# Three pairs of feed-forward input units by seven block products each, with the second matrix's chunks between them

## The chip, the cores and the metric

One core of one Trainium2 chip runs the kernel. The metric is the device time of one execution in microseconds. A core has a matrix engine (TensorE, PE in the rows; PEld is its weight loading), a vector engine (VectorE, DVE), a scalar engine (ScalarE, ACT), GpSimd (POOL), a queue that issues transfers (SyncE, SP), an on-chip memory SBUF, and a small memory PSUM of eight banks into which TensorE writes its sums.

## The reference

x has 256 rows (tokens) of 1024 columns, in float32. Two layers follow each other, each with a feed-forward, a mixer (attention in the first layer, retention in the second) and a second feed-forward:

```python
def _swiglu(xn, w_in, w_out):
    a, b = jnp.split(xn @ w_in, 2, axis=-1)
    return (jax.nn.silu(a) * b) @ w_out
...
        h = x + 0.5 * _swiglu(_rms(x, ffn1_norm[i]), ffn1_w_in[i], ffn1_w_out[i])
        xn = _rms(h, mix_norm[i])
...
        h = h + m.astype(h.dtype)
        x = h + 0.5 * _swiglu(_rms(h, ffn2_norm[i]), ffn2_w_in[i], ffn2_w_out[i])
```

In a feed-forward `w_in` is 1024 x 5632 (2816 columns for a, 2816 for b) and `w_out` 2816 x 1024. The four feed-forwards are called f0 to f3 here: f0, attention, f1, f2, retention, f3.

## The kernel before, in words

**Precision.** Each float32 operand of a large product is split in two numbers of TensorE's faster format: hi, its rounding, and lo, the rest. A product of two operands is three matmuls: hi by hi, lo by hi, hi by lo (`mm_tokens`, L280). A matmul has 128 rows of the left operand held in the array, and 512 columns of the right one streamed through it.

**Weights.** The class `Weights` (L96) keeps a list of loads in the order in which they are used. A load is one `raw` tile of 128 x 2048 float32 (1 MB), brought by SP. ACT rounds it to `hi` (L162), in two pieces of 128 x 1024, and DVE subtracts to get `lo` (L169). There are four raw, four hi and four lo buffers. Loads run ahead of the splits (L128), and splits at most four parts ahead of the parts that TensorE has freed (L151). While matmuls are issued, the object `Flow` (L61) counts the nanoseconds that TensorE should take, and issues one split piece every 800 of them (L174) unless `urgent` is set, which is so around a norm. A step of side work is a generator that yields the nanoseconds after which it goes on. The program's order is what these counts give; the scheduler that compiles the program may still put instructions of an engine in another order, where their inputs allow (only SP's order and the opening's are held, L801 and L486).

**A feed-forward** (`ffn`, L437) has eleven units of 256 columns of a and the 256 columns of b that belong to them. A unit takes two parts: rows 0 to 511 and 512 to 1023 of its 512 columns of `w_in`. For each of two groups of 128 tokens it sums 24 matmuls in one PSUM bank (`ps_f`), after which ACT takes the silu (`st_f`, L442) and DVE multiplies (`gt_f`, L444). Two transposes on TensorE (`ptg_f`, L305) and another split give `hT`, the left operand of the second matrix. When all units are done, `out_proj` (L384) goes through the second matrix in eleven chunks of 256 rows, one part each; four banks (`y`) hold the 256 x 1024 result, 24 matmuls a chunk. The last two chunks are taken together, tile by tile, so that the residual (L423), the squares (L345), the root on POOL (L355), the scaling (`xs`, L369), four transposes per 512 columns and the split into `xn` (`norm_transpose`, L361) can begin before the last tile is summed. The next stage's first matmuls follow.

The diff touches `Weights`, the plan of loads (`plan_ffn`, L243), `norm_transpose`, `out_proj`, `ffn` and the calls at the end (L795).

Of the kernel before, what the change touches and what calls it, by code (L numbers as in the profile page):

```python
# [15 lines left out]
ALU = mybir.AluOpType  # L16
# [79 lines left out]
class Weights:  # L96

    RAW, PARTS, PACE = 4, 4, 800  # L100

    def __init__(self, nc, pool, flow):
        self.nc, self.pool, self.flow = nc, pool, flow
        self.specs, self.raws, self.parts = [], [], []
        self.taken = self.freed = self.next = 0
        self.todo, self.rounded = [], []
        flow.idle = self.paced

    def add(self, src, shape, pieces):
        self.specs.append((src, shape, pieces))  # L110

    def cols(self, w, c0, n, k0=0, nk=KD, pieces=2):
        src = w[k0 * P : (k0 + nk) * P, c0 : c0 + n].rearrange("(k p) c -> p k c", p=P)
        self.add(src, [nk, n], pieces)

    def pair_cols(self, w, c0, c1, n, k0, nk, pieces=2):
# [4 lines left out]
        self.add(src, [nk, 2 * n], pieces)  # L121

    def rows(self, w, k0):
        src = w[k0 * P : (k0 + 2) * P, :].rearrange("(k p) c -> p k c", p=P)
        self.add(src, [2, w.shape[1]], 2)

    def load(self, most=1000):
        while len(self.raws) < min(len(self.specs), len(self.parts) + self.RAW, most):  # L128
            i = len(self.raws)
            src, shape, pieces = self.specs[i]  # L130
            raw = self.pool.tile([P] + shape, F32, tag="raw", name=f"raw{i}", bufs=self.RAW)
            n = shape[0] // (pieces if pieces > 2 else 1)
            parts = src if isinstance(src, list) else [src]
# [6 lines left out]
            self.raws.append(raw)  # L140

# [6 lines left out]
    def round(self):  # L148
        if not self.todo:
# [4 lines left out]
            _, shape, pieces = self.specs[i]  # L154
# [7 lines left out]
        self.nc.scalar.copy(self.parts[i][0][:, ks, :], self.raws[i][:, ks, :])  # L162
        return True

    def remain(self):
        i, ks, last = self.rounded.pop(0)
        hi, lo = self.parts[i]
        raw = self.raws[i]
        self.nc.vector.tensor_tensor(lo[:, ks, :], raw[:, ks, :], hi[:, ks, :], ALU.subtract)  # L169
        if last:  # L170
            self.raws[i] = None
            self.load()
# [32 lines left out]
def trunk_kernel(ctx: ExitStack, tc: tile.TileContext, io, out: bass.AP):  # L205
# [36 lines left out]

    def plan_ffn(w_in, w_out):  # L243
        for j in range(FF // 256):
            for i in range(2):
                pieces = 2 if len(wts.specs) > 1 else 4
                wts.pair_cols(w_in, j * 256, FF + j * 256, 256, 4 * i, 4, pieces)
        for c in range(FF // 256):
# [25 lines left out]
    def mm(ps, lhsT, rhs, start, stop):  # L274
        nc.tensor.matmul(ps, lhsT=lhsT, rhs=rhs, start=start, stop=stop)  # L275
# [4 lines left out]
    def mm_tokens(ps, t, part, k0, nk, first, last):  # L280

        hi, lo = part
        for k in range(nk):
# [4 lines left out]
            mm(ps, xh, lo[:, k, :], False, last and k == nk - 1)  # L288

# [36 lines left out]
    def sum_halves(out_ap, ps, name):  # L326
        rest = work.tile([P, T], F32, tag="rest", name=f"rest_{name}")
# [33 lines left out]
    def norm_transpose(t, dst, gain, name):  # L361
# [3 lines left out]
        xs = []  # L365
        for n in range(2):
            x = work.tile([P, 512], F32, tag="xs", name=f"xs_{name}{t}{n}")
# [462 lines left out]
```

## Time and profile before

| | us |
|---|---|
| three runs, median (lowest to highest) | 1081.95 (1081.24 to 1082.28) |
| the profiled execution | 1081.91 |
| its span, first to last instruction | 1080.1 |
| TensorE busy | 1070.1 |
| VectorE busy | 622.6 |
| ScalarE busy | 512.5 |

A profile is one execution. In its rows L162 is line 162 of the kernel, `hi<-raw` an instruction that writes hi and reads raw, x24 a count, and what stands in brackets the idle time before it and what ended it. Matmuls overlap, so the mean of one is longer than the distance from start to start; the distance is what counts for the time. Some matmul records are missing from a trace. The granted clock is 1.00 at TensorE's full 2.4 GHz.

### The profile page before, as it was taken

What the parts mean: (1) busy time and instruction counts of PE and PEld (TensorE: products, weight loads), DVE (VectorE), ACT (ScalarE), POOL (GpSimd) and SP (SyncE); (2) the same over time, 40 slices, a digit from 0 to 9 for tenths busy, and PEclk for the clock granted to TensorE, in tenths of its full rate; (3) what the DMA queues carried; (4) which work ended last, traced back from release to release, by engine and by line L of the source; (5) the groups of instructions that cost most, each with busy time, mean ns of one, the idle gap of its engine ahead of it and who ended that gap; (6) DMA issues with size and microseconds to landing.
All of it is one profiled execution on the core that took longest, in us unless ns stands there. A gap on an engine that the chain in (4) does not pass through costs nothing.

```text
span 1080.1 us, 12936 instructions
## 1 busy us (share of the span) xinstructions
PE 1070.1 (99%) x5016; PEld 878.1 (81%) x5016; DVE 622.6 (58%) x848; ACT 512.5 (47%) x789; POOL 37.2 (3%) x38
## 2 busy tenths in 40 slices
PE   8999999999999999999999999999999999999998
PEld 6888888877778888888888888888888888888887
DVE  5646544778875655546554554656655556565541
ACT  6545443557664444434444543445544444454430
POOL 0000000122010000000000000000000000000000
PEclk9999999999999999999999999999999999999999
DMA  8965555473337565564756465476456556656531
GB/s 282 284 194 159 205 186 194 138 242 124 121 118 243 170 203 173 194 195 137 234 181 203 162 201 193 142 242 205 154 177 217 156 156 198 191 163 205 181 115 39
DMA packets 135440, 196.47 MB, mean 182 GB/s; under 512 B 5330, under 2 KB 104658, under 8 KB 135379
## 3 DMA queue, kind: packets, MB, share of 16 engines
q1 hardware_dynamic: 135378, 195.65, 56.5%
q8 instruction: 39, 0.64, 0.2%
q14 instruction: 23, 0.18, 0.0%
HBM read 194.58 MB, written 1.05 MB: 181 GB/s over the span
## 4 chain that ended last, share of the span: by engine, by line
PE 94%; DVE 3%; POOL 1%; issue 1%; SPq 0%; DMA 0%; ACT 0%; POOLq 0%; ACTq 0%
PE ps_f L275 44%; PE pj L275 13%; PE y_f3o L275 6%; PE y_f1o L275 6%; PE y_f0o L275 6%; PE y_f2o L275 6%; PE pqk L275 4%; PE y_rto L275 4%; PE ptg_f L305 2%; PE y_dao L275 2%; DVE lo L169 1%; PE rpo L686 1%; PE po L611 0%; PE sT L665 0%; DMA raw<-in_ffn_w_in_dram 0%
## 5 line engine op out<-in xcount | busy, mean ns | idle before, releaser
L169 DVE TENSOR_TENSOR lo<-raw,hi 128x1024 fp32r<-128x1024 f32 (+1 forms) x364 | 430.5, 1209 | 242.0 <-ACT hi L162 241.3
L162 ACT CAST hi<-raw 128x1024 fp32r<-128x1024 f32 (+1 forms) x364 | 367.4, 1043 | 256.6 <-PE ps_f L275 95.2
L275 PE MATMUL ps_f<-hi,xn_in 128*128 128x512 f32 x352 | 113.4, 402 | 1.4 <-ACT xn_in L323 1.4
L275 PE MATMUL ps_f<-hi,xn_dao 128*128 128x512 f32 x352 | 111.1, 396 | 0.0
L275 PE MATMUL ps_f<-hi,xn_rto 128*128 128x512 f32 x352 | 111.1, 396 | 0.0
L275 PE MATMUL ps_f<-hi,xn_f1o 128*128 128x512 f32 x352 | 111.1, 396 | 0.0
L442 ACT ACTIVATE st_f<-ps_f 128x256 f32<-128x256 f32 x88 | 33.3, 378 | 134.2 <-PE ps_f L275 134.2
L444 DVE TENSOR_TENSOR gt_f<-ps_f,st_f 128x256 f32<-128x256 f32 x88 | 36.9, 420 | 87.5 <-ACT st_f L442 87.5
L275 PE MATMUL pj<-hi,xn_f2o 128*128 128x512 f32 x256 | 81.1, 393 | 0.0
L275 PEld LDWEIGHTS ps_f<-hi,xn_in 128*128 128x128 f32 x352 | 66.0, 192 | 15.3 <-ACT xn_in L323 1.8
L275 PEld LDWEIGHTS ps_f<-hi,xn_dao 128*128 128x128 f32 x352 | 64.7, 188 | 12.7
L275 PEld LDWEIGHTS ps_f<-hi,xn_f1o 128*128 128x128 f32 x352 | 64.7, 188 | 12.7
L275 PEld LDWEIGHTS ps_f<-hi,xn_rto 128*128 128x128 f32 x352 | 64.7, 188 | 12.7
L275 PE MATMUL ps_f<-lo,xn_in 128*128 128x512 f32 x176 | 69.8, 397 | 0.0
L275 PE MATMUL ps_f<-lo,xn_f1o 128*128 128x512 f32 x176 | 68.9, 392 | 0.0
L275 PE MATMUL ps_f<-lo,xn_rto 128*128 128x512 f32 x176 | 68.9, 391 | 0.0
L275 PE MATMUL ps_f<-lo,xn_dao 128*128 128x512 f32 x176 | 68.9, 391 | 0.0
L275 PE MATMUL pj<-hi,xn_f0o 128*128 128x512 f32 x192 | 62.6, 400 | 0.0
L275 PE MATMUL y_f3o<-hi,hT_f 128*128 128x512 f32 (+1 forms) x220 | 56.9, 348 | 0.0
L275 PEld LDWEIGHTS pj<-hi,xn_f2o 128*128 128x128 f32 x256 | 48.1, 188 | 9.7
L275 PE MATMUL y_f0o<-hi,hT_f 128*128 128x512 f32 x176 | 54.8, 391 | 0.0
L275 PE MATMUL y_f1o<-hi,hT_f 128*128 128x512 f32 x176 | 54.7, 391 | 0.0
(189 smaller groups left out, 1519.7 us busy)
## 6 DMA issues: line engine op xcount, KB each, us to landing
raw<-in_ffn_w_in_dram SPq DMA_DIRECT2D x172, 512.0 KB, 5.0
raw<-in_ffn_w_out_dram SPq DMA_DIRECT2D x44, 1024.0 KB, 4.9
raw<-in_rt_w_in_dram SPq DMA_DIRECT2D x24, 1024.0 KB, 5.2
raw<-in_da_w_in_dram SPq DMA_DIRECT2D x12, 1024.0 KB, 5.1
raw<-in_rt_w_out_dram SPq DMA_DIRECT2D x8, 1024.0 KB, 5.0
raw<-in_da_w_out_dram SPq DMA_DIRECT2D x4, 1024.0 KB, 4.9
raw<-in_ffn_w_in_dram SPq DMA_DIRECT2D x16, 128.0 KB, 3.7
g_in_ffn_norm_dram<-in_ffn_norm_dram SPq DMA_DIRECT2D x3, 512.0 KB, 4.1
```

What stands on the lines that cost most here:

```text
L162: self.nc.scalar.copy(self.parts[i][0][:, ks, :], self.raws[i][:, ks, :])
L169: self.nc.vector.tensor_tensor(lo[:, ks, :], raw[:, ks, :], hi[:, ks, :], ALU.subtract)
L275: nc.tensor.matmul(ps, lhsT=lhsT, rhs=rhs, start=start, stop=stop)
L305: nc.tensor.transpose(pt[:, j * P : (j + 1) * P], src[:, j * P : (j + 1) * P], ident)
L442: nc.scalar.activation(s, ps[:, :256], AF.Silu)
L444: nc.vector.tensor_tensor(g, ps[:, 256:], s, ALU.mult)
L686: nc.tensor.matmul(po[t], lhsT=lhs[:, cs], rhs=v[rhs][:, vt, :], start=first and lhs is ph and rhs == 0, stop=last and lhs is pl,)
```

## The change

Six of the eleven units of a feed-forward are taken in pairs, (1,2), (4,5) and (7,8). The product of a pair, 256 tokens by 1024 rows by two units' columns, is seen as a two by two block product, and made from seven products of blocks (128 tokens by 512 rows by 512 columns, 12 matmuls each) instead of eight. For that:

- `sums_transpose` makes four sums and differences of blocks of the normalised x, transposes and splits them. It runs after the norm ahead of f0, f1, f2 and f3. To keep the unscaled tiles, `xs` moves into the pool of 13 large blocks.
- A pair loads the same four raw tiles, but makes seven parts of them (`seven`): four as loaded, three from sums, which DVE forms in place by four adds of 128 x 2048 ahead of the second and the fifth part. A raw tile can be kept for several parts, so loads are now counted by the raw tiles that are live.
- Two products of the seven go on in a bank whose earlier content a first reader has taken (`more`), and DVE adds or subtracts the products to the four results, with copies in SBUF, ahead of silu and multiplication.
- A unit's four transposes go to one bank and one split (`finish_unit`).
- The chunks of the second matrix no longer wait for all units: the list `ITEMS` gives the order of units (u), pairs (s) and chunks (o). The four banks of the result are held from the first chunk on. The last two chunks are taken as before.

```diff
+    def seven(self, w, ci, cj, n):
+        b11 = self.pair(w, *ci, n, 0, 4)
+        b12 = self.pair(w, *cj, n, 0, 4)
+        b22 = self.pair(w, *cj, n, 4, 4)
+        b21 = self.pair(w, *ci, n, 4, 4)
+        self.part(b11, keep=True)
+        self.part(b11, [(b12, b22, ALU.add), (b11, b12, ALU.add)], keep=True)
+        self.part(b21, keep=True)
+        self.part(b12)
+        self.part(b11, [(b21, b11, ALU.add), (b11, b22, ALU.subtract)])
+        self.part(b21)
+        self.part(b22)
...
-        while len(self.raws) < min(len(self.specs), len(self.parts) + self.RAW, most):
+        while len(self.raws) < min(len(self.loads), most) and self.live < self.RAW:
...
+            raw, sums, keep, pieces = self.specs[i]
+            for to, by, op in sums:
+                self.nc.vector.tensor_tensor(self.raws[to], self.raws[to], self.raws[by], op)
+            shape = self.loads[raw][1]
...
+        if last and not keep:
+            self.raws[raw] = None
+            self.live -= 1
...
+    ITEMS = (
+        "u0 s1,2 o0 u3 o1 o2 s4,5 o3 u6 o4 o5 s7,8 o6 u9 o7 u10 o8"
+    ).split()
...
+            if item[0] == "u":
+                for i in range(2):
+                    pieces = 4 if first and item == "u0" and i == 0 else 2
+                    wts.part(wts.pair(w_in, *cs[0], 256, 4 * i, 4, pieces), pieces=pieces)
+            elif item[0] == "s":
+                wts.seven(w_in, *cs, 256)
+            else:
+                wts.rows(w_out, 2 * js[0])
...
+    def mm_product(ps, left, part, more=False):
+        hi, lo = part
+        for k in range(KD // 2):
+            lh, ll = left(k)
+            mm(ps, lh, hi[:, k, :], k == 0 and not more, False, more)
+            mm(ps, ll, hi[:, k, :], False, False, more)
+            mm(ps, lh, lo[:, k, :], False, k == KD // 2 - 1, more)
+        wts.free()
...
+            if sums is not None:
+                sums.append(flow.spawn(sums_transpose(sums, name)))
+    def sums_transpose(sums, name):
+        x0, x1 = xs[0], xs[1]
+        yield 1500
+        ab = blk(f"ab_{name}", F32, [2, 512])
+        cd = blk(f"cd_{name}", F32, [2, 512])
+        nc.vector.tensor_tensor(ab[:, 0, :], x1[:, 1, :], x1[:, 0, :], ALU.subtract)
+        nc.vector.scalar_tensor_tensor(
+            ab[:, 1, :], ab[:, 0, :], -1.0, x0[:, 0, :], ALU.mult, ALU.subtract
+        )
+        nc.vector.tensor_tensor(cd[:, 0, :], x0[:, 0, :], x1[:, 0, :], ALU.subtract)
+        nc.vector.scalar_tensor_tensor(
+            cd[:, 1, :], x0[:, 1, :], -1.0, ab[:, 1, :], ALU.mult, ALU.subtract
+        )
+        for i, src in ((1, ab), (2, cd), (0, ab), (3, cd)):
+            yield 2000
+            pt = transposes(f"ps_{name}{i}", src[:, i % 2, :], 4)
+            s = blk(f"sum_{name}{i}", F32R, [2, 4, P])
+            split_to(s[:, 0], s[:, 1], pt.rearrange("p (k c) -> p k c", c=P))
+            sums[i] = s
...
+        def finish_unit(j, gs, wait):
+            yield wait
+            pt = bank(f"ptg_{name}{j}")
+            for i in range(2):
+                for t in range(NT):
+                    at = (2 * i + t) * P
+                    nc.tensor.transpose(
+                        pt[:, at : at + P], gs[t][:, i * P : (i + 1) * P], ident
+                    )
+            flow.now += 300
+            hT[j] = blk(f"hT_{name}{j}", F32R, [2, 2, T])
+            split_to(hT[j][:, :, 0, :], hT[j][:, :, 1, :], pt.rearrange("p (i c) -> p i c", c=T))
...
+        def units(i, j):
+            flow.join(sums[-1])
+            tag = f"{name}{i}"
+            def x(t, k0):
+                ts, tl = slice(t * P, (t + 1) * P), slice(T + t * P, T + (t + 1) * P)
+                return lambda k: (xn[0][:, k0 + k, ts], xn[0][:, k0 + k, tl])
+            def s(n):
+                return lambda k: (sums[n][:, 0, k, :], sums[n][:, 1, k, :])
+            def tmp(what):
+                return work.tile([P, 512], F32, tag="xs", name=f"{what}_{tag}", bufs=3)
+            b1, b2 = bank(f"b1_{tag}"), bank(f"b2_{tag}")
+            mm_product(b1, x(0, 0), wts.take())
+            p1 = tmp("p1")
+            nc.scalar.copy(p1, b1)
+            mm_product(b2, s(1), wts.take())
+            u2 = tmp("u2")
+            nc.vector.tensor_tensor(u2, b2, p1, ALU.add)
+            mm_product(b1, x(0, 4), wts.take(), True)
+            g11 = gate(f"{tag}_11", b1)
+            mm_product(b2, s(2), wts.take(), True)
+            u3 = tmp("u3")
+            nc.vector.tensor_tensor(u3, b2, p1, ALU.add)
+            b3, b4 = bank(f"b3_{tag}"), bank(f"b4_{tag}")
+            mm_product(b3, s(0), wts.take())
+            nc.vector.scalar_tensor_tensor(p1, b3, -1.0, u3, ALU.mult, ALU.subtract)
+            g22 = gate(f"{tag}_22", p1)
+            mm_product(b4, x(1, 4), wts.take())
+            nc.vector.tensor_tensor(u3, b4, u3, ALU.add)
+            g21 = gate(f"{tag}_21", u3)
+            done[i] = flow.spawn(finish_unit(i, (g11, g21), 3000))
+            mm_product(b3, s(3), wts.take(), True)
+            nc.vector.scalar_tensor_tensor(u2, b3, -1.0, u2, ALU.mult, ALU.subtract)
+            g12 = gate(f"{tag}_12", u2)
+            done[j] = flow.spawn(finish_unit(j, (g12, g22), 4000))
...
+        y = OutProj(FF // P, src, 0.5, f"{name}o", next_gain, last, next_sums)
+        for item in ITEMS:
+            js = [int(j) for j in item[1:].split(",")]
+            {"u": unit, "s": units, "o": y.chunk}[item[0]](*js)
+        return y.finish()
```

Not shown: the new class `OutProj` holds what `out_proj` did, by chunk; other stages call it as before; two work buffers get other names or counts.

## Rows read from the trace of the kernel before

**Rows 1.** The profile page: busy time by engine, and the chain that ended last.

```profile
PE 1070.1 (99%) x5016; PEld 878.1 (81%) x5016; DVE 622.6 (58%) x848; ACT 512.5 (47%) x789; POOL 37.2 (3%) x38
...
PE 94%; DVE 3%; POOL 1%; issue 1%; SPq 0%; DMA 0%; ACT 0%; POOLq 0%; ACTq 0%
```

**Rows 2.** Busy time by stretch, f1's two matrices (engines, clock, DMA, GB/s).

```profile
322.50:444.20 121.70, 121.70 (x556) 99.74 (x555) 67.77 (x87) 58.36 (x87) 0.00 (x0) 1.00 0.62 195
444.20:510.60 66.40, 65.97 (x300) 54.28 (x299) 34.87 (x38) 27.97 (x37) 2.01 (x2) 1.00 0.55 174
```

**Rows 3.** The chain in order of time: start us, us, what, f0 and f1.

```profile
18.35 8.19 PE ps_f L275 x36
...
449.94 51.73 PE y_f1o L275 x228
```

**Rows 4.** TensorE in order of time, f2's start (start us, us).

```profile
504.60 0.62 PE L275 MATMUL ps_f<-hi,xn_f1o 128*128 128x512 f32 x2
...
509.27 0.63 PE L305 MATMUL pt_f1o<-ident,xs_f1o 128*128 128x128 f32 x4 [0.43 <-DVE xs_f1o L369]
509.65 0.48 PE L275 MATMUL ps_f<-hi,xn_f1o 128*128 128x512 f32 x1
509.97 0.60 PE L305 MATMUL pt_f1o<-ident,xs_f1o 128*128 128x128 f32 x4
```

**Rows 5.** VectorE in order of time, last chunks of f1.

```profile
488.28 2.36 DVE L169 TENSOR_TENSOR lo<-raw,hi 128x1024 fp32r<-128x1024 f32 x2 [3.08 <-ACT hi L162]
```

**Rows 6.** VectorE by line and shape (busy us, mean ns, then idle before).

```profile
L169 DVE TENSOR_TENSOR lo<-raw,hi 128x1024 fp32r<-128x1024 f32 x356 | 425.4, 1221 | 242.0 <-ACT hi L162 241.3 <-PE ptg_f L305 0.5
...
L444 DVE TENSOR_TENSOR gt_f<-ps_f,st_f 128x256 f32<-128x256 f32 x88 | 36.9, 420 | 87.5 <-ACT st_f L442 87.5
...
L169 DVE TENSOR_TENSOR lo<-raw,hi 128x512 fp32r<-128x512 f32 x8 | 5.1, 685 | 0.0
...
L369 DVE SCALAR_TENSOR_TENSOR xs_f1o<-h,r_f1o,g_in_ffn_norm_dram 128x512 f32<-128x512 f32 x4 | 2.8, 749 | 1.1 <-POOL r_f1o L355 1.1
...
L423 DVE SCALAR_TENSOR_TENSOR h<-y_f1o,h 128x512 f32<-128x512 f32 x4 | 2.8, 688 | 1.7 <-PE y_f1o L275 1.6
```

**Rows 7.** ScalarE by line and shape.

```profile
L162 ACT CAST hi<-raw 128x1024 fp32r<-128x1024 f32 x356 | 362.7, 1052 | 253.7 <-PE ps_f L275 95.2 <-PE y_f1o L275 30.7 <-PE y_f0o L275 30.6
...
L641 ACT COPY v<-pj 128x512 f32<-128x512 f32 x4 | 2.3, 575 | 0.5 <-PE pj L275 0.5
```

**Rows 8.** The profile page: DMA issues (KB each, us to landing).

```profile
raw<-in_ffn_w_in_dram SPq DMA_DIRECT2D x172, 512.0 KB, 5.0
```

**Rows 9.** VectorE in order of time at f2's start.

```profile
504.80 0.69 DVE L423 SCALAR_TENSOR_TENSOR h<-y_f1o,h 128x512 f32<-128x512 f32 x1
505.41 1.22 DVE L169 TENSOR_TENSOR lo<-raw,hi 128x1024 fp32r<-128x1024 f32 x1
506.58 0.21 DVE L363 TENSOR_SCALAR v_f1o<-ssp_f1o 128x1 f32<-128x1 f32 x1
506.71 1.22 DVE L169 TENSOR_TENSOR lo<-raw,hi 128x1024 fp32r<-128x1024 f32 x1
508.37 1.42 DVE L369 SCALAR_TENSOR_TENSOR xs_f1o<-h,r_f1o,g_in_ffn_norm_dram 128x512 f32<-128x512 f32 x2 [0.44 <-POOL r_f1o L355]
```

**Rows 10.** ScalarE in order of time, opening.

```profile
25.79 1.99 ACT L162 CAST hi<-raw 128x1024 fp32r<-128x1024 f32 x2
...
28.30 1.05 ACT L162 CAST hi<-raw 128x1024 fp32r<-128x1024 f32 x1 [0.23 <-DMA raw<-in_ffn_w_in_dram]
```

**Rows 11.** TensorE in order of time, opening.

```profile
10.70 1.52 PE L275 MATMUL ps_f<-hi,xn_in 128*128 128x512 f32 x2 [1.39 <-ACT xn_in L323]
12.02 0.63 PE L275 MATMUL ps_f<-lo,xn_in 128*128 128x512 f32 x1
...
13.30 0.63 PE L275 MATMUL ps_f<-lo,xn_in 128*128 128x512 f32 x1
...
16.85 0.39 PE L275 MATMUL ps_f<-lo,xn_in 128*128 128x512 f32 x1
```

More of the change, by code (lines that the diff above doesn't have):

```diff
@@ L103, in __init__ @@
         self.nc, self.pool, self.flow = nc, pool, flow
-        self.specs, self.raws, self.parts = [], [], []
-        self.taken = self.freed = self.next = 0
+        self.loads, self.specs = [], []
+        self.raws, self.parts = [], []
+        self.live = self.taken = self.freed = self.next = 0
         self.todo, self.rounded = [], []
@@ L405, in out_proj, with chunk @@
+                mm(y, ah, lo[:, k, cs], False, kk == self.nk - 1, more)
+        def chunk(self, c):
+            if self.ys is None:
+                self.ys = {
+                    (t, i): bank(f"y_{self.name}{t}{i}") for t in range(NT) for i in range(2)
+                }
             part = wts.take()
             for t in range(NT):
-                for c0, n in pieces[t]:
-                    chunk_mms(t, c0, n, c, part)
-            wts.free()
-        tails = [wts.take() for _ in range(TAIL)]
@@ new lines, in chunk, with finish @@
+            wts.free()
+        def finish(self):
+            name, last = self.name, self.last
+            pieces = [[(0, 512), (512, 512)] for _ in range(NT)]
+            if last:
+                pieces[-1][1:] = [(512, 256), (768, 256)]
+            tails = [wts.take() for _ in range(TAIL)]
+            tasks = []
+            if not last:
+                xn[0] = new_xn(name)
+            for t in range(NT):
+                for c0, n in pieces[t]:
+                    if not last and (t, c0) == (0, 512):
+                        flow.urgent += 1
+                    for i, part in enumerate(tails):
+                        self.mms(t, c0, n, self.nk // 2 - TAIL + i, part)
+                        if t == NT - 1 and c0 + n == D:
+                            wts.free()
+                    cs = slice(c0, c0 + n)
+                    y = self.ys[t, c0 // 512][:, c0 % 512 : c0 % 512 + n]
+                    nc.vector.scalar_tensor_tensor(
+                        h[t][:, cs], y, self.coef, h[t][:, cs], ALU.mult, ALU.add
+                    )
+                    if last:
+                        nc.sync.dma_start(out[0, t * P : (t + 1) * P, cs], h[t][:, cs])
+                    else:
+                        square_half(t, c0 // 512, name)
+                if not last:
+                    halves = [self.gain[:, :512], self.gain[:, 512:]]
+                    tasks.append(
+                        flow.spawn(norm_transpose(t, xn[0], halves, name, self.sums))
+                    )
+            return tasks
@@ L486, in attention @@
+        return y.finish()
+    def attention(before, next_gain, next_sums):
         dist = const.tile([P, 384], F32, name="dist")
```

184 lines of the change are left out of this document (78 added, 106 removed).

## The prediction

> **What bounds the kernel now.** I read the page first, for the busy shares and the chain of waits. The reader sees TensorE 99% busy and 94% of the chain; VectorE (DVE) is busy 58% and ScalarE (ACT) 47% of the span [rows 1]. Then the table by stretches: in one whole feed-forward (its first matrix 121.7 us, its second 66.4 us) TensorE never waits for long, the granted clock is 1.00, DVE is busy 67.8 + 34.9 = 102.6 us of 188.1, and the DMA share is 0.62 and 0.55 [rows 2]. So the bound is TensorE's instruction count. The pieces of the chain give its price: 228 matmuls in 51.73 us, 0.227 us each [rows 3]. DVE has 85 us per feed-forward to spare, but not everywhere.
>
> The sum is made against the profiled execution's own 1081.91 us (span 1080.1); the median of the runs, 1081.95, is the same time.
>
> **TensorE's part.** A pair of units costs 2 x 2 x 8 x 3 = 96 matmuls now and 7 x 12 = 84 after. Three pairs in four feed-forwards: 144 fewer, x 0.227 = 32.7 us gone. Added are four sums of x per feed-forward, each a group of four transposes. At the norm such a group takes 0.38 us until the next matmul starts, and that matmul then takes 0.32 instead of 0.227 to the next start: 0.47 us [rows 4]. 16 x 0.47 = 7.5 us. The second matrix's chunks are only moved: the same 264 matmuls. A unit's four transposes go in one group instead of two pairs, which I cost at nothing. **Net on TensorE: 32.7 - 7.5 = 25.2 us less**, to 1056.7 if all else stays covered.
>
> **DVE's part.** Operations on DVE overlap a little: two lo pieces of 1.22 us take 2.36 us together [rows 5], so one costs 1.14, and I take 0.08 off every duration. A pair has seven parts instead of four: three more, six lo pieces, 6.8 us. Then four adds of 128x2048. No row has that width. The rows of 512 and 1024 (685 and 1221 ns) give 536 ns per 512 columns, so 2.29 us, 2.21 back to back [rows 6]; the ends are 1.22 (it runs twice as fast) and 2.44 (two of 1024), and I take the slope, since both rows are the same kind of operation. The Trainium skill (VectorE: DVE Perf Modes, The perf-mode tier table) gives 2293 ns for such an add; no run here shows one, and by that figure the sum would be the same. Five combinations of 128x512, most from PSUM, as the residual's 688 ns [rows 6]: 3.1 us. Per feed-forward that is 3 x (6.8 + 8.8 + 3.1) = 56 us; the x sums add four operations like lo's 685 and xs's 749 ns of 512 columns, and four splits [rows 6], 5.0 us. DVE goes from 103 to about 163 us in a feed-forward that would last 182. On average it fits; the question is where it does not.
>
> **ACT** gains 18 hi pieces of 1052 ns and seven copies like v's 575 ns [rows 7], 23 us per feed-forward, on an engine half idle: nothing. **DMA**: the same bytes, transfers of 512 KB that land in 5.0 us [rows 8]. Four raw buffers are all held from a pair's fourth load until its fourth part is split. Then the next loads start, and four parts with two adds on DVE (13.5 us) lie between the first of them and the next chunk's need: nothing. **PSUM**: the second matrix holds four banks from its first chunk on; a pair needs the other four, each freed by a DVE or ACT read. I cost it with DVE.
>
> **The first pair of each feed-forward.** The program lets parts run only four ahead (hi and lo have four buffers each). During the last two chunks, with both still held, only the next unit 0's two parts can be made; DVE idles 3.08 us before each pair of pieces there [rows 5]. The pair's parts start when the norm does. The order on an engine is the scheduler's, not the program's: two lo pieces stand around v, though the program issues them after the norm's transposes [rows 9]. So I assume that DVE fills its gaps, and that the first add (of two raws already there) slips into the idle time of the last chunks.
>
> For f2's start (504.8 us in [rows 9]), DVE must do before the seventh product can start: the norm 3.3 (h, v, two xs, two splits); unit 0's gates 0.7 [rows 6]; x sums and splits 5.0; seven parts 16.0; three adds 6.6; two sums from PSUM, one subtraction, a gate and a split 2.8; and the next chunk's part, issued before that subtraction, 2.3. That is 36.7, with 0.7 of waits it ends at 542.2. TensorE would be there at 504.6 (unit 0's first matmul) + 48 x 0.227 + 0.4 (its wait at the norm [rows 4]) + 0.9 + 0.5 + 1.9 (transposes) + six products of 2.72 = 535.5. **DVE is 6.7 us late.** If the chunk's part, the gates and the splits are put later it is some 2.5. I take 6 for each of three feed-forwards, as the trace shows no order kept by need.
>
> f0 has its raws later: the pieces that are unit 2's now, the third and fourth raw of the first pair after, reach ACT at 25.8 and 28.3 us [rows 10]. From 25.8: adds 4.4, ACT's first piece after them 1.0, parts two to seven 13.7, adds 4.4, the small ones 2.8, the chunk 2.3 = 28.6, to 54.4. TensorE ends unit 0 near 26 (the chain's 36 matmuls to 26.5 [rows 3]) and would reach the seventh product at 26 + 1.9 + 16.3 = 44.2. Late by 10; between 7 and 12.
>
> **The other eight pairs.** They come after two chunks or a unit and chunks. From the release of the first part (8.6 us into the unit) to the pair's end TensorE has 33 us, DVE 31: adds 8.8, eight parts 18.2, small ones 4. The second pair of adds needs no hi or lo buffer and can be made before the first product. So I take 0.5 us each, 4. An add in place of a lo piece between v and xs delays the norm by about 1 us at f1, f2 and f3: 3.
>
> **Sum:** 1081.9 - 25.2 + 10 + 3 x 6 + 4 + 3 = 1091.7; I say **1091**, chance 0.38, its own range 1083 to 1099.
>
> **Rivals.**
> *Covered (faster), 0.35.* The scheduler puts what is needed first, or the adds are cheaper than the slope: 2.5 us at three pairs and 7 at f0, nothing else: 1081.9 - 25.2 + 14.5 = 1071; with all covered 1057. For it: DVE's 85 us to spare [rows 2], and gaps that the scheduler filled [rows 9]. Against: four buffers allow no more parts ahead.
> *The adds stay in place (slower), 0.15.* In the eight later pairs part five's adds are made only where the program issues them, in the second product. Then 4.4 us of adds stand ahead of the sum that frees the bank of the fourth product, and part seven ahead of the one that frees the seventh's: 3 us each, 24 more: 1115. It decides if adds lie after the pair's first product on DVE. Against: [rows 9].
> *The clock falls (slower), 0.12.* At the opening TensorE had waited 1.4 us, and its matmuls then stood 0.427 us apart (three from 12.02 to 13.30), the pitch of the 1.2 GHz level, nearly twice the usual 0.227; by 16.85 a matmul was short again [rows 11]. Some 14 matmuls lie between, x 0.2 = 2.8 us lost. A wait of 3 us or more in the first pair could do that again: 4 x 2.8 = 11 more, 1102. Against: the norm's waits of 0.4 us were followed by matmuls at full pitch [rows 4]. The Trainium skill (TensorE: Matmul & The Clock Gate, What's actually happening) says that "the default state is throttled, and activity releases the throttle"; the opening agrees, with 0.427 us per matmul, though the granted clock of the profile reads 1.00 throughout.
>
> **The numbers.** About 0.2% (2 us) is what a measurement of this kernel can tell from no change. Faster by more: nearly all of the first rival and a little of the forecast, 0.35. Within: the forecast's lower edge and the first rival's upper one, 0.12. Slower: the rest, 0.53. Signs are mixed, so the range is wide: from 1066, inside the covered case, to 1112, past the clock's and short of the adds' case.
>
> **What would show it.** The profile after should have 144 fewer matmuls and 64 more transposes, the adds near 2.29 us, DVE near 870 us busy, and idle time of TensorE that it did not have, released by DVE, inside the first pair of each feed-forward, with matmuls following that still stand 0.227 us apart. I am wrong if TensorE waits there for under 3 us (covered), if the waits lie as much in the second and third pairs (adds in place), if matmuls of 0.43 us appear after a wait (clock), or if TensorE waits for a DMA.

## The result, and the profile after

The changed kernel takes 1105.71 us (median of four runs, 1104.51 to 1107.75) against 1082.0: ratio 1.0222, interval 1.0204 to 1.0240, 23.8 us slower. Forecast were 1091 and a range of 1066 to 1112: the direction came out, the loss is 2.6 times the 9 us forecast.

The page after (busy time by engine; the chain; VectorE's adds) answers to [rows 1]:

```profile
PE 1057.8 (96%) x4882; PEld 859.6 (78%) x4882; DVE 853.8 (77%) x1014; ACT 592.5 (54%) x843; POOL 37.3 (3%) x38
...
PE 51%; DVE 29%; DMA 9%; ACT 5%; issue 4%; POOL 1%; SPq 1%; POOLq 0%; ACTq 0%; DVEq 0%
...
L181 DVE TENSOR_TENSOR raw<-raw,raw 128x2048 f32<-128x2048 f32 x48 | 109.7, 2285 | 3.1 <-DMA raw<-in_ffn_w_in_dram 2.7
```

TensorE has lost its place as the only bound: 51% of the chain instead of 94%, with VectorE at 29%. Its own busy time fell by 12 us, not by 25, and it is idle 45.7 us (1103.5 - 1057.8) where it was idle 10. The adds take the 2.29 us taken for them, VectorE's 854 us are near the 870 forecast. The page counts 134 matmuls and transposes fewer, where 144 less and 64 more make 80. The other 54 are in f3's second matrix: the kernel before made one result tile there in two halves of 256 columns in all eleven chunks, the change does so in the last two only. That is the same number of columns, so little time. The list of waits (us in total, times, longest) says for whom TensorE waits now, and in its last line how long ScalarE waits for loads:

```profile
PE ptg_f L555 <- DVE g_f L546: 11.1, 12, 1.4
PE b_f L320 <- DVE u_f L600: 8.1, 4, 2.5
PE ps_in L360 <- DVE ab_in L449: 6.2, 1, 6.2
...
ACT hi L190 <- DMA raw<-in_ffn_w_in_dram: 32.2, 23, 2.4
```

TensorE's three largest waits are new, and VectorE releases all three: a gate of a pair (the product of silu and the other half, `g_f`; 12 times in twelve pairs), the sum that frees the bank of the fourth product (in the first pair of each feed-forward), and the x sums in f0. The gate is in every pair the one made from the sixth product (`g21`, after L611). No wait of TensorE ends with a load of weights, but ScalarE's waits for them are 32.2 us, where they were 5.3; what that does is seen further below. The second wait is seen in VectorE's order in f1's first pair:

```profile
350.29 2.28 DVE L181 TENSOR_TENSOR raw<-raw,raw 128x2048 f32<-128x2048 f32 x1
...
353.09 2.28 DVE L181 TENSOR_TENSOR raw<-raw,raw 128x2048 f32<-128x2048 f32 x1
355.29 0.68 DVE L600 TENSOR_TENSOR u_f<-b_f,p_f 128x512 f32<-128x512 f32 x1
```

Part five's two adds stand ahead of the sum `u_f` (L600). TensorE starts the last matmul of the third product at 353.18 and then has to wait for that sum; and after the wait it runs at half speed for a while. The same place in TensorE's order, and the stretches behind it (granted clock, DMA share and GB/s at the end of a row):

```profile
353.18 0.39 PE L320 MATMUL b_f<-lo,xn_dao 128*128 128x512 f32 x1
356.03 0.95 PE L320 MATMUL b_f<-hi,sum_dao 128*128 128x512 f32 x2 [2.46 <-DVE u_f L600]
```

```profile
357.50:360.00 2.50, 2.50 (x7) 1.88 (x7) 2.50 (x4) 2.50 (x3) 0.00 (x0) 0.54 0.03 5
360.00:362.50 2.50, 2.50 (x12) 2.06 (x11) 2.50 (x3) 2.50 (x4) 0.00 (x0) 1.00 0.90 269
```

Seven matmuls were started in the 2.5 us where the clock was 0.54, twelve where it was 1.00. In f2 the same wait (2.48 us) is followed by the lower clock too, in f3 it is not:

```profile
934.75 0.73 PE L320 MATMUL b_f<-hi,sum_rto 128*128 128x512 f32 x2 [2.46 <-DVE u_f L600]
...
935.00:937.50 2.50, 2.50 (x12) 2.04 (x12) 2.32 (x4) 2.50 (x4) 0.00 (x0) 1.00 0.00 0
```

In f0 the adds stand ahead of the first of the four sums of x (L448 to L453), and TensorE stands still from 28.95 to 35.15:

```profile
23.88 4.61 DVE L181 TENSOR_TENSOR raw<-raw,raw 128x2048 f32<-128x2048 f32 x2
...
31.88 0.69 DVE L448 TENSOR_TENSOR ab_in<-xs_in 128x512 f32<-128x512 f32 x1
...
34.32 0.69 DVE L449 SCALAR_TENSOR_TENSOR ab_in<-ab_in,xs_in 128x512 f32<-128x512 f32 x1
```

The lengths of the stages, from the first transpose of one norm to that of the next (f0 from the start of the span, f3 to its end), with two experiments beside them:

| us | f0 | attention | f1 | f2 | retention | f3 |
|---|---|---|---|---|---|---|
| before | 198.2 | 115.4 | 188.1 | 188.1 | 195.5 | 194.9 |
| after | 210.3 | 116.2 | 191.7 | 190.9 | 196.0 | 198.3 |
| after, no adds | 196.5 | 115.9 | 182.1 | 181.9 | 195.5 | 187.8 |
| after, no adds in the first pairs | 199.0 | 115.3 | 186.6 | 183.9 | 195.5 | 190.3 |

### The profile page after: what moved, and what is told of

Read it like the earlier page. It is cut to its first block, busy times and chain, and to the rows that moved or that the text cites. A ratio compares the mean times of both kernels' runs of the same rounds, so it can differ in the third digit from the quotient of the medians.

```text
span 1103.5 us, 12875 instructions
## 1 busy us (share of the span) xinstructions
PE 1057.8 (96%) x4882; PEld 859.6 (78%) x4882; DVE 853.8 (77%) x1014; ACT 592.5 (54%) x843; POOL 37.3 (3%) x38
## 4 chain that ended last, share of the span: by engine, by line
PE 51%; DVE 29%; DMA 9%; ACT 5%; issue 4%; POOL 1%; SPq 1%; POOLq 0%; ACTq 0%; DVEq 0%
DVE lo L197 16%; PE ps_f L320 14%; PE pj L320 12%; DMA raw<-in_ffn_w_in_dram 9%; DVE raw L181 7%; PE pqk L320 4%; ACT hi L190 4%; PE y_f2o L320 3%; PE y_f3o L320 3%; PE y_rto L320 3%; PE y_f0o L320 3%; PE y_f1o L320 3%; PE ptg_f L555 2%; PE b_f L320 1%; DVE g_f L546 1%
## 5 line engine op out<-in xcount | busy, mean ns | idle before, releaser
L197 DVE TENSOR_TENSOR lo<-raw,hi 128x1024 fp32r<-128x1024 f32 (+1 forms) x434 | 512.4, 1213 | 84.3 <-ACT hi L190 84.1
L190 ACT CAST hi<-raw 128x1024 fp32r<-128x1024 f32 (+1 forms) x434 | 434.6, 1045 | 212.9 <-DVE raw L181 53.7
L181 DVE TENSOR_TENSOR raw<-raw,raw 128x2048 f32<-128x2048 f32 x48 | 109.7, 2285 | 3.1 <-DMA raw<-in_ffn_w_in_dram 2.7
L320 PE MATMUL y_f2o<-hi,hT_f 128*128 128x512 f32 x176 | 56.6, 396 | 0.7 <-ACT hT_f L378 0.7
L320 PE MATMUL ps_f<-hi,xn_in 128*128 128x512 f32 x160 | 52.1, 405 | 2.9 <-ACT xn_in L378 1.6
L320 PE MATMUL ps_f<-hi,xn_rto 128*128 128x512 f32 x160 | 50.5, 394 | 0.7 <-DVE xn_rto L379 0.7
L320 PE MATMUL ps_f<-hi,xn_dao 128*128 128x512 f32 x160 | 50.5, 394 | 0.7 <-DVE xn_dao L379 0.7
L320 PE MATMUL ps_f<-hi,xn_f1o 128*128 128x512 f32 x160 | 50.5, 394 | 0.7 <-DVE xn_f1o L379 0.7
L320 PE MATMUL pj<-lo,xn_f2o 128*128 128x512 f32 x128 | 49.8, 389 | 0.0
L320 PE MATMUL pqk<-xn_f2o,hi 128*128 128x512 f32 x128 | 44.6, 398 | 0.0
L555 PE MATMUL ptg_f<-ident,g_f 128*128 128x128 f32 x176 | 30.2, 284 | 11.1 <-DVE g_f L546 11.1
```

The source lines that it names most:

```text
L181: self.nc.vector.tensor_tensor(self.raws[to], self.raws[to], self.raws[by], op)
L190: self.nc.scalar.copy(self.parts[i][0][:, ks, :], self.raws[self.specs[i][0]][:, ks, :])
L197: self.nc.vector.tensor_tensor(lo[:, ks, :], self.raws[raw][:, ks, :], hi[:, ks, :], ALU.subtract)
L555: nc.tensor.transpose(pt[:, at : at + P], gs[t][:, i * P : (i + 1) * P], ident)
```

## The experiments

### Which part of the change costs the time

**The adds left out.**

```diff
-            for to, by, op in sums:
-                self.nc.vector.tensor_tensor(self.raws[to], self.raws[to], self.raws[by], op)
```

> Leaves out VectorE's 48 adds of 128x2048; the three sum parts of a pair are then plain copies of raw tiles, everything else stays (parts, products, transposes, order). Theory (VectorE's adds stand ahead of what TensorE needs, in the first pair and in f0's opening, and the clock falls after those waits): the wait of 2.5 us before the fourth product and the matmuls at half speed after it go, and so does most of the 6.2 us wait for the x sums in f0: 1105.7 - 4 x 4 - 6 - 3 x 0.8 = about 1082, between 1074 and 1090. Rival (the interleaved chunks, with their late hidden tiles and four banks held, cost the time): the adds are not what TensorE waits for, 1100 or more.

Measured: 1060.64 us, ratio to before 0.9811 (0.9797 to 0.9826). The theory holds, and the time lies below its range (1074 to 1090): without the adds the change is a gain, 45 us below the changed kernel. The page and the wait that was 11.1:

```profile
PE 1044.0 (99%) x4882; PEld 855.0 (81%) x4882; DVE 749.7 (71%) x966; ACT 594.9 (56%) x843; POOL 37.2 (4%) x38
...
PE ptg_f L553 <- DVE g_f L544: 2.3, 4, 1.1
```

The two spans differ by 43.7 us. Of that TensorE's idle time is 29.9 (45.7 against 15.8) and its busy time 13.8 (1057.8 against 1044.0), with the same matmuls. At most some 10 us of the second are the clock: its mean over the span is 0.991 with the adds (0.009 x 1103.5 = 9.9) and 1.000 without. For the rest no row is shown; it may be matmuls that run out and start again around the added waits, since one alone counts for 0.39 us and one in a row for 0.227.

**The chunks between the units, without pairs.**

```diff
+        "u0 u1 u2 o0 u3 o1 o2 u4 u5 o3 u6 o4 o5 u7 u8 o6 u9 o7 u10 o8"
...
+                    pieces = 4 if first and item == "u0" else 2
...
-            if sums is not None:
+            if False:
```

> No pairs and no sums of x: eleven plain units, the second matrix's chunks put between them as in the change, four transposes of a unit in one group, and both first parts of f0 in four pieces as before. The same work as the kernel before in another order. Theory: the chunks between the units cost next to nothing, within 3 us of the kernel before (1079 to 1085), waits of TensorE at the hidden tiles' transposes under 3 us in all. Rival (the chunks between the units cost the time): 1090 or more.

Measured: 1078.81 us, ratio 0.9978 (0.9968 to 0.9987). That is 0.2 us under the theory's range and 2.4 under the kernel before as measured beside it (1081.20). The rival falls: the chunks between the units cost nothing.

**The pairs, without the chunks between the units.**

```diff
+        "u0 s1,2 u3 s4,5 u6 s7,8 u9 u10 o0 o1 o2 o3 o4 o5 o6 o7 o8"
```

> The three pairs stay, the second matrix's chunks go back behind all units. Theory: the first pair's wait before its fourth product, the half-speed matmuls after it and f0's opening stay as they are, and only some of the wait for the last tile of a pair is saved: 1097 to 1106. Rival (chunks between the units): the pairs alone are a gain, 1060 to 1080.

Measured: 1147.16 us, ratio 1.0620 (1.0593 to 1.0647). Both expectations miss. The waits show why:

```profile
PE ptg_f L555 <- DVE g_f L546: 31.7, 13, 4.5
PE b_f L320 <- DVE u_f L600: 14.1, 11, 2.5
```

With the chunks gone from between them, the pairs come with one plain unit between two, and the fourth product waits in nearly every pair (11 times). So the chunks are what gives VectorE time to catch up; they are worth 41 us here.

**The adds on GpSimd.**

```diff
-                self.nc.vector.tensor_tensor(self.raws[to], self.raws[to], self.raws[by], op)
+                self.nc.gpsimd.tensor_tensor(self.raws[to], self.raws[to], self.raws[by], op)
```

> The 48 adds of 128x2048 are made by GpSimd instead of VectorE. Theory: VectorE is free for what TensorE waits for, but GpSimd's add is slower than 2.29 us and stands ahead of the second part in the first pair; if it takes under 5 us: 1085 to 1100, with TensorE's wait moved to the pair's second product. If the two engines slow each other down in SBUF, VectorE's lo pieces grow beyond 1.22 us and the time is above 1106. Rival (chunks): no change, 1103 to 1108.

Measured: 1214.06 us, ratio 1.1226 (1.1204 to 1.1248). Two groups, VectorE's lo pieces and GpSimd's adds, then TensorE's largest wait and ScalarE's order at one of its places, in f0's second pair:

```profile
L197 DVE TENSOR_TENSOR lo<-raw,hi 128x1024 fp32r<-128x1024 f32 x430 | 589.7, 1397 | 193.9 <-ACT hi L190 193.6
...
L181 POOL TENSOR_TENSOR raw<-raw,raw 128x2048 f32<-128x2048 f32 x48 | 235.2, 4899 | 475.5 <-DMA raw<-in_ffn_w_in_dram 215.7 <-DVE lo L197 119.7 <-DVE h L514 61.8
...
PE b_f L320 <- ACT p_f L597: 66.5, 8, 9.7
...
111.76 1.04 ACT L190 CAST hi<-raw 128x1024 fp32r<-128x1024 f32 x1 [11.04 <-POOL raw L181]
112.71 0.58 ACT L597 COPY p_f<-b_f 128x512 f32<-128x512 f32 x1
```

GpSimd's add is twice as long, and the lo pieces grew from 1218 to 1397 ns, 430 x 0.18 = 77 us, of the 110 that the adds had taken from VectorE. The time lies above 1106, as was expected if the two engines slow each other down. The largest wait is another one: in the eight later pairs TensorE waits 66.5 us for ScalarE's copy of the first product, and in the rows shown that copy stands behind a rounding which waits 11.04 us for GpSimd's adds. GpSimd is no place for them here.

### Which adds, and what waits for them

**The adds of the first pair alone left out.**

```diff
+        self.part(b11, [(b12, b22, ALU.add), (b11, b12, ALU.add)] if adds else (), keep=True)
...
+        self.part(b11, [(b21, b11, ALU.add), (b11, b22, ALU.subtract)] if adds else ())
...
+                wts.seven(w_in, *cs, 256, item != "s1,2")
```

> Leaves out the four adds of the first pair alone, in each feed-forward (16 of 48 adds); the sum parts of that pair are then plain copies. All 48 were worth 45 us (1105.7 against 1060.6). Theory (the first pair pays, since VectorE has just done the norm and the sums of x): more than two thirds of the 45 go with a third of the adds, 1070 to 1078. Rival (each pair pays alike for its adds): a third, 1088 to 1093.

Measured: 1072.78 us, ratio 0.9927 (0.9912 to 0.9943). A third of the adds is worth 32.9 of the 45.1 us: the first pairs pay. The other 12.1 are the adds of the second and third pairs. Against the run without any adds TensorE waits 6.4 us longer for the gates (8.7 against 2.3) and is busy 4.7 us longer (1048.7 against 1044.0), which is nearly all of the 10.8 us between the spans (1070.6 and 1059.8):

```profile
PE 1048.7 (98%) x4882; PEld 855.4 (80%) x4882; DVE 818.7 (76%) x998; ACT 592.3 (55%) x843; POOL 37.2 (3%) x38
...
PE ptg_f L555 <- DVE g_f L546: 8.7, 10, 1.8
...
453.92 0.55 PE L555 MATMUL ptg_f<-ident,g_f 128*128 128x128 f32 x3 [1.84 <-DVE g_f L546]
...
454.60:458.00 3.40, 3.40 (x10) 2.63 (x9) 3.40 (x6) 1.21 (x3) 0.00 (x0) 0.50 0.98 348
```

The last two rows are the longest of these waits and the stretch behind it: behind 1.84 us of waiting the clock fell to 0.50 here.

What makes the gate late in the later pairs is not VectorE's work alone. f2's second pair in the changed kernel: the chain first, then ScalarE, VectorE and TensorE in order of time:

```profile
597.81 4.63 DVE lo L197 x4
602.88 6.91 DMA raw<-in_ffn_w_in_dram
...
609.89 1.05 ACT L190 CAST hi<-raw 128x1024 fp32r<-128x1024 f32 x1 [2.21 <-DMA raw<-in_ffn_w_in_dram]
610.85 0.41 ACT L544 ACTIVATE s_f<-p_f 128x256 f32<-128x256 f32 x1
...
611.29 0.43 DVE L546 TENSOR_TENSOR g_f<-p_f,s_f 128x256 f32<-128x256 f32 x1 [1.65 <-ACT s_f L544]
...
614.97 0.55 PE L555 MATMUL ptg_f<-ident,g_f 128*128 128x128 f32 x3 [1.27 <-DVE g_f L546]
```

A load is issued when VectorE's lo pieces have freed a raw tile, and lands 6.91 us later. ScalarE waits for it with a rounding of the next unit's weights, and a silu of the pair stands behind that. So VectorE is idle for 1.65 us, and everything behind, with the gate that TensorE waits for, comes that much later. All eight later pairs show it: VectorE is idle for 0.9 to 1.8 us until that silu is done, in each of them longer than TensorE then waits (0.5 to 1.4 us). How much a fifth raw buffer, or the silu ahead of the rounding, would give back was not tried.

**The fourth product's bank freed by ScalarE.**

```diff
-            nc.vector.tensor_tensor(u2, b2, p1, ALU.add)
+            nc.scalar.copy(u2, b2)
+            nc.vector.tensor_tensor(u2, u2, p1, ALU.add)
```

> Only the second product's way out of PSUM: ScalarE copies it to SBUF and so frees the bank for the fourth product, and VectorE makes the sum from there, when it comes to it. Theory (the fourth product of the first pair waits 2.5 us because the sum stands behind part five's two adds on VectorE, and the half-speed matmuls follow from that wait): the wait of 8.1 us in four feed-forwards goes, with some 1.5 us of slow matmuls each in f0, f1, f2: 1092 to 1098. Rival (VectorE is behind by that much, and the next thing it owes TensorE comes late instead, a lo piece of part five or the fifth product's bank): 1103 to 1107.

Measured: 1106.69 us, ratio 1.0233 (1.0218 to 1.0249), no gain. The wait for `u_f` left the list, and others came:

```profile
PE ptg_f L555 <- DVE g_f L546: 11.4, 13, 2.2
...
PE b_f L320 <- DVE lo L197: 2.9, 3, 1.0
```

TensorE's idle time is 43.4 us instead of 45.7, and its busy time 3.5 us longer. The rival holds here: VectorE is behind with all its work in the first pair, and the operation named in the wait is only the first one that shows it.

**f0's first parts in four pieces again.**

```diff
-                    pieces = 4 if first and item == "u0" and i == 0 else 2
+                    pieces = 4 if first and item == "u0" else 2
```

> Only f0's opening: both parts of unit 0 come in four transfers and are rounded in four pieces, as in the kernel before. Theory (the opening lost time to the coarser pieces, which stand ahead of the norm of the second 128 tokens, and to the first pair's pieces that moved in among them): the second norm 3.4 us earlier, f0 3 to 6 us shorter, 1099.5 to 1102.5. Rival (the wait for the adds sets f0's start whatever the pieces): no change, within 1 us of 1105.7.

Measured: 1101.89 us, ratio 1.0188 (1.0172 to 1.0203): 3.8 us less, as the theory has it; between the two profiled executions it is 2.1 (spans of 1103.5 and 1101.4), with f0 2.8 us shorter. Yet the wait of 6.2 us for the x sums did not vanish, it went three products further, to the sum behind the next adds:

```profile
46.85 1.19 PE L320 MATMUL b_f<-hi,sum_in 128*128 128x512 f32 x2 [6.33 <-DVE u_f L600]
```

### What stands behind a pair, and ahead of it

**The last transposes later.**

```diff
-            done[i] = flow.spawn(finish_unit(i, (g11, g21), 3000))
+            done[i] = flow.spawn(finish_unit(i, (g11, g21), 6000))
...
-            done[j] = flow.spawn(finish_unit(j, (g12, g22), 4000))
+            done[j] = flow.spawn(finish_unit(j, (g12, g22), 9000))
```

> Only the delays after which a pair's last transposes are put into TensorE's order: 6000 and 9000 ns of matmuls instead of 3000 and 4000, so they come behind the chunk or inside the unit that follows. Theory (TensorE waits there for the last gate, which stands behind adds and lo pieces on VectorE): the wait of 11.1 us in all goes to under 3 us and with it some of the half-speed matmuls, 1091 to 1098. Rival (VectorE is simply short of time there, and what TensorE does not wait for at the transposes it waits for at the next lo piece): 1102 to 1107.

Measured: 1097.07 us, ratio 1.0141 (1.0126 to 1.0156), 8.6 us less; the total is as the theory has it, but 8.1 of the 11.1 us of waits are still listed, so the account by waits was not met:

```profile
PE ptg_f L555 <- DVE g_f L546: 8.1, 8, 2.4
```

**The first pair later.**

```diff
+        "u0 u3 o0 s1,2 o1 o2 o3 s4,5 u6 o4 o5 o6 s7,8 u9 o7 u10 o8"
```

> Only the order of units and chunks: units 0 and 3 and the first chunk come ahead of the first pair, and one more chunk ahead of the second and the third pair. Theory (the first pair comes before VectorE has caught up with the norm, the sums of x and the parts): first-pair waits and the 6.2 us for the sums of x go, the waits at the pairs' last transposes stay or shrink: 1078 to 1090. Rival (a pair's parts and adds are limited by four raw, hi and lo buffers, so that a pair costs the same wherever it stands): 1098 to 1106.

Measured: 1087.80 us, ratio 1.0064 (1.0047 to 1.0080): 17.9 us less, for the theory.

**Late, four pieces and later transposes together.**

```diff
+        "u0 u3 o0 s1,2 o1 o2 o3 s4,5 u6 o4 o5 o6 s7,8 u9 o7 u10 o8"
...
+                    pieces = 4 if first and item == "u0" else 2
...
+            done[i] = flow.spawn(finish_unit(i, (g11, g21), 6000))
...
+            done[j] = flow.spawn(finish_unit(j, (g12, g22), 9000))
```

> The late first pair, the four pieces in f0 and the later last transposes together, in the order u0 u3 o0 s1,2 o1 o2 o3 s4,5 u6 o4 o5 o6 s7,8 u9 o7 u10 o8. They gave 17.9, 3.8 and 8.6 us alone. Theory: the gains overlap in the first pair, some 22 to 26 us remain, 1080 to 1084. Rival (they are independent): 1075.

Measured: 1086.98 us, ratio 1.0054 (1.0037 to 1.0072). Both expectations miss: nothing was added to the late order's gain. f1's first pair, behind its sixth product:

```profile
370.38 0.70 PE L320 MATMUL b_f<-hi,sum_dao 128*128 128x512 f32 x2 [1.48 <-DVE p_f L608]
...
375.17 0.55 PE L555 MATMUL ptg_f<-ident,g_f 128*128 128x128 f32 x3 [1.78 <-DVE g_f L546]
376.39 1.62 PE L320 MATMUL y_f1o<-hi,hT_f 128*128 128x512 f32 x5 [0.67 <-ACT hT_f L378]
```

The next item behind this pair is chunk 1, which needs unit 1, the pair's own output. TensorE stands still at the seventh product's bank, at the gate of the sixth and at its split, 3.9 us; no other work was put in between.

**A unit behind each pair, and three chunks ahead of the next.**

```diff
+        "u0 u3 o0 s1,2 u6 o1 o2 o3 s4,5 u9 o4 o5 o6 s7,8 u10 o7 o8"
...
+                    pieces = 4 if first and item == "u0" else 2
...
+            done[j] = flow.spawn(finish_unit(j, (g12, g22), 6000))
```

> Units, pairs and chunks in the order u0 u3 o0 s1,2 u6 o1 o2 o3 s4,5 u9 o4 o5 o6 s7,8 u10 o7 o8, so that a plain unit follows each pair and three chunks stand ahead of the next; both first parts of f0 in four pieces; the last transposes of a pair after 3000 and 6000 ns. Theory (VectorE needs time around each pair to get ahead, and a unit after the pair takes the last gate off TensorE's path): the waits at the pairs' transposes under 3 us in all, 1066 to 1076, faster than both kernels. Rival (what is left is the pair itself, its 28 us of VectorE in 19 us of TensorE with parts only four ahead): 1078 to 1086.

Measured: 1063.39 us, ratio 0.9831 (0.9819 to 0.9844): faster than both kernels, and the theory's value is bettered. The same pair in TensorE's order:

```profile
362.37 0.62 PE L320 MATMUL ps_f<-hi,xn_dao 128*128 128x512 f32 x2
...
364.79 0.62 PE L320 MATMUL b_f<-hi,sum_dao 128*128 128x512 f32 x2
...
370.20 0.55 PE L555 MATMUL ptg_f<-ident,g_f 128*128 128x128 f32 x3 [0.70 <-DVE g_f L546]
```

After the sixth product come ten matmuls of the plain unit (`ps_f`), and only then the seventh product, without a wait: the scheduler filled the time in which VectorE was late with work that needs nothing from it. The page, and f1 as one stretch (span, TensorE, its weight loads, VectorE, then ACT, POOL, clock, DMA):

```profile
PE 1045.0 (98%) x4882; PEld 854.5 (81%) x4882; DVE 853.2 (80%) x1016; ACT 593.0 (56%) x845; POOL 37.2 (4%) x38
...
311.50:494.20 182.70, 181.40 (x832) 148.75 (x833) 160.19 (x167) 106.60 (x137) 2.02 (x2) 1.00 0.58 193
```

VectorE has 160.2 us of work in f1's 182.7, the load the change gave it, and nothing of it is taken away; the longest wait of TensorE for the pairs' operands is 1.6 us. What has changed is where TensorE stands when VectorE is behind. Three things were changed at once here (the order, the delay of the last transposes, f0's pieces), so the gain is theirs together.

**Five parts ahead.** The same order with five hi and lo buffers, and nine large blocks instead of thirteen.

```diff
+    RAW, PARTS, PACE = 4, 5, 800
...
+    blkp = ctx.enter_context(tc.tile_pool(name="blkp", bufs=9))
```

> The spread order as above with five hi and lo buffers instead of four, and nine large blocks instead of thirteen to make room. Theory (four parts ahead are too few to hide a pair's excess of VectorE work over TensorE's): 3 to 8 us below the spread order alone. Rival (the raw buffers, four, are what limits it, or nine blocks make new waits): not below it.

Measured: 1063.23 us, ratio 0.9830 (0.9817 to 0.9842), the same time as the spread order. With that order, four hi and lo buffers are not what limits. The number of raw buffers stayed four.

**Only the unit moved behind the pair.**

```diff
+        "u0 s1,2 u3 o0 o1 o2 s4,5 u6 o3 o4 o5 s7,8 u9 o6 o7 u10 o8"
...
+            done[j] = flow.spawn(finish_unit(j, (g12, g22), 6000))
```

> The change's order with one swap: the plain unit that stood behind the first chunk comes directly behind each pair, u0 s1,2 u3 o0 o1 o2 s4,5 u6 o3 o4 o5 s7,8 u9 o6 o7 u10 o8, and the last transposes of a pair after 3000 and 6000 ns. The first pair stays where it was, two parts behind the norm. Theory A (what matters is what TensorE has to do behind a pair: a unit's matmuls need nothing of the pair and can be put ahead of its last product): most of the late order's gain comes with it, 1078 to 1090. Theory B (what matters is the time VectorE has ahead of the first pair): the first pair's wait of 2.5 us, its slow matmuls and f0's loss stay, and only the 11.1 us of waits at the transposes go: 1091 to 1097.

Measured: 1086.12 us, ratio 1.0044 (1.0028 to 1.0061), 19.6 us less: in theory A's range. But theory B's remainder is there too: the waits at the last transposes are gone from the list, while those of the first pair and of f0 stand unchanged.

```profile
PE b_f L320 <- DVE u_f L600: 8.6, 5, 2.5
PE ps_in L360 <- DVE ab_in L449: 6.2, 1, 6.2
```

So both count: what TensorE has to do behind a pair (19.6 us, together with the later transposes, whose delay alone, at 6000 and 9000, gave 8.6), and VectorE's time ahead of the first pair, with f0's pieces (22.7 us more, to the spread order's 1063.4).

### The clock by itself

The kernel before, with a wait of TensorE in four units of each feed-forward:

```diff
+    LATE = {2: 0, 4: 1, 6: 3, 8: 5}
...
+                start = len(issued(tc)) if t == 0 else start
...
+                if t == 0 and j in LATE:
+                    w = work.tile([P, 512], F32, tag="xs", name=f"late_{name}{j}")
+                    nc.scalar.copy(w, ps)
+                    for _ in range(LATE[j]):
+                        nc.vector.tensor_tensor(w, w, w, ALU.max)
+                    transposes(f"pl_{name}{j}", w, 1)
+                if t == 1 and j in LATE:
+                    keep_order(tc, start, mybir.EngineType.PE)
```

> The kernel before with a wait of TensorE put into units 2, 4, 6 and 8 of each feed-forward: ScalarE copies the unit's first sum, VectorE makes 0, 1, 3 and 5 operations of 128x512 on the copy, one after the other, and TensorE must transpose the result before it may go on. That is some 0.8, 1.5, 2.9 and 4.3 us of waiting (0.575 for the copy, 0.7 for each operation, and what lo piece is under way), 38 us in all. Theory (a wait of 2.5 us or more drops the clock, and the matmuls behind it take some 1.6 us more): the stretches behind the waits of 0.8 and 1.5 us show 1.00, those behind 2.9 and 4.3 us show 0.5, 8 times 1.6 = 13 us on top of the waits: about 1133. Rival (the half-speed matmuls of the changed kernel have another cause): no more than the waits, about 1120.

Measured: 1139.95 us, ratio 1.0538 (1.0523 to 1.0554). The profiled span is 1135.9 us, of which the waits listed for these transposes are 39.7 (37.0 for VectorE, 2.7 for ScalarE where no operation of VectorE stands between):

```profile
PE 1085.9 (96%) x5032; PEld 885.9 (78%) x5032; DVE 645.5 (57%) x884; ACT 520.2 (46%) x805; POOL 37.2 (3%) x38
...
PE pl_f L305 <- DVE late_f L474: 37.0, 12, 4.6
```

TensorE is busy 15.8 us longer than before; 16 transposes more, at some 0.08 each, are 1.3 of that. Of the other 14.5, 11.8 are matmuls at half speed: of the 16 places, those after waits of 0.68 us (four) and 1.49 (four) have the next 25 matmuls and transposes started within 5.4 us; of the four after 3.15 us two are slow; all four after 4.60 are; and the six slow ones take 1.2 to 2.5 us longer. A wait of 3.15 with each outcome, then the 2.5 us behind these two and behind one of 4.60:

```profile
410.74 0.45 PE L305 MATMUL pl_f<-ident,late_f 128*128 128x128 f32 x1 [3.15 <-DVE late_f L474]
...
613.25 0.30 PE L305 MATMUL pl_f<-ident,late_f 128*128 128x128 f32 x1 [3.15 <-DVE late_f L474]
```

```profile
410.74:413.24 2.50, 2.50 (x8) 2.01 (x9) 0.00 (x0) 0.31 (x1) 0.00 (x0) 0.50 0.00 0
...
613.25:615.75 2.50, 2.50 (x13) 2.06 (x14) 0.42 (x1) 0.37 (x1) 0.00 (x0) 1.00 0.05 17
641.01:643.51 2.50, 2.50 (x8) 2.01 (x9) 0.00 (x0) 0.31 (x1) 0.00 (x0) 0.50 0.02 7
```

The theory holds in kind: waits of TensorE are followed by half speed here too, without any change to the products, and the rival falls. The total is 7 us above the 1133 expected, and a wait of some 3 us decides nothing by itself: the same 3.15 us left the clock at 1.00 twice.

## Why the prediction was right and wrong

**TensorE's part: right.** Without the adds the kernel is at 1060.6; the sum's floor was 1056.7. f1 and f2 take 182.1 and 181.9 us there, against 188.1 - 8.2 + 1.9 = 181.8 by the prediction's terms (36 matmuls less, four groups more). "The same 264 matmuls" was not so in f3 (330 before, 276 after), which changed little: with the chunks between the units and no pairs, f3 is 0.8 us shorter than before, f1 and f2 0.6.

**VectorE's load: right.** 2285 ns an add, 854 us busy, 160.3 in f1 against "about 163". The Trainium skill (VectorE: DVE Perf Modes, The perf-mode tier table) gave 2293 ns; the trace agrees, with 2285.

**The first pairs: right in size, wrong in place.** Their adds are worth 11.3 us in f0, 5.1, 7.0 and 8.0 in f1 to f3 (second row of the table minus the last), against 10 and 6 + 1 forecast. But the step had VectorE late at the seventh product. TensorE stood already at the fourth, and in f0 before the first, because adds stand ahead of a sum that TensorE needs sooner: the order within the engine decided, which the sum of VectorE's work could not show. And up to some 8 of the 32.9 us are not waiting but clock (mean 0.991 against 0.998), which the sum left out: that the size came out is in part luck.

**The other eight pairs: the step that failed.** "So I take 0.5 us each, 4", because VectorE has 31 us of work in 33. Their adds cost 12.1 us. The step weighed the work of two engines, and the prediction put ScalarE and the loads at "nothing". The trace shows the wait elsewhere: TensorE waits for the gate of the sixth product, and in all eight pairs VectorE comes to it late because it stood idle itself, 0.9 to 1.8 us, for a silu behind a rounding that waited for a load. Loads were taken at 5.0 us; the one shown is issued behind VectorE's lo pieces and takes 6.91. That the adds delay the loads by keeping VectorE and the raw tiles longer fits these rows, but no run shows it by itself. The prediction also asked what stands ahead of a pair and not what follows it. In the spread order, with a plain unit behind the pair, the same VectorE load fits, though ScalarE still waits 24.3 us for loads of the two matrices.

**f0's pieces: not seen.** The diff shows four pieces for the first part only. The second part's two coarser pieces, and the first pair's that then move into the opening, cost 3.8 us by the run that undoes it (2.1 by the profiled executions), which the sum had at nothing.

These make the difference: 8.1 for the eight pairs, 3.8 for the pieces and 1.9 for the first pairs with the norm (32.9 against 28 + 3) are 13.8 of the 14.0 us by which 1105.7 lies above the sum's 1091.7. Each is from leaving one part out, so overlaps between them are not told apart, and the kernel before itself lay between 1081.2 and 1082.0 beside these runs.

**The rivals.** *The clock falls*, given 0.12, happened beside the forecast's waits: at most some 10 us of the time, against 11 worked out. It is not added to the terms above; it lies within them. The bound of 3 us for it was too high: a wait of 2.46 us in f1 was followed by it, and one of 1.84 in the run without the first pairs' adds. *The adds stay in place* came true in another place than named: in the first pairs the adds stand ahead of the sum; in the later pairs too (an add ends at 596.6 in f2's second pair, and the sum follows), but no wait of TensorE at the fourth product is seen there. *Covered* is what the spread order makes true.

## What to carry to other kernels

When work goes from a full engine to a half-idle one, don't compare sums of work over a stage: take the point where the full engine next needs a result, and list what stands ahead of it in the other engine's order, and in the order of each engine that this one waits for, down to the load. Then look at what the full engine could do meanwhile: independent work directly behind the dependent stretch let the same VectorE load cost little here (1063.4 us against 1060.6 without the adds in the change's own order), and a version 24 us slower became one 18 us faster by its order, later transposes and f0's four pieces. And price each wait of TensorE with the slow matmuls that may follow it.

## What the runs showed of the hardware that was not expected

In the kernel before with waits put in, TensorE's granted clock stayed at 1.00 after 0.68 and 1.49 us in all eight places, fell to the 1.2 GHz level after 3.15 in two places of four and after 4.60 in all four. In the other runs the length of one wait did not decide it either: 2.46 us in f1 of the changed kernel were followed by the fall and 2.46 us in f3 were not, and 1.84 us in the run without the first pairs' adds were. Each is from one execution. An add of 128x2048 took GpSimd 4899 ns (the mean of 48) against VectorE's 2285, and while it ran VectorE's own pieces became longer (1218 to 1397 ns in the mean). The Trainium skill (GPSIMD Engine Reference, Elementwise — side-by-side cycle accounting) gives 4497 ns for that add by itself; the trace shows more, beside a busy VectorE.
